# A gathered prefix sum and projection: gathers that convert to FP16 themselves, and stores of two pairs

## The chip, the cores and the metric

The kernel runs on one core of a Trainium2 chip. A time is the time of one execution on the device in microseconds (us); of several runs the median is given. The profile is of one further execution. PE is TensorE, DVE is VectorE, ACT is ScalarE, POOL is GpSimd and SP is SyncE.

## What is computed

```
x: (16, 4096, 512) float32    indices: (16, 2048) int64, sorted    w: (512, 512) float32
gathered = x[b_idx, indices, :]
cs = np.cumsum(gathered, axis=1)
out = np.matmul(cs, w)                      # (16, 2048, 512) float32
```

In each of 16 batches, 2048 rows of 512 numbers are picked, summed up from the first row to each row, and multiplied by one matrix. 67 MB are read by the gathers and 67 MB are written.

## The kernel before, in words

The rows are cut into 256 tiles of 128 rows, 16 to a batch. Two tiles that follow each other make a pair. A tile passes through six steps, each on one engine:

- **gather** (line 127, issued at line 137): POOL issues an indirect DMA. It takes the 128 row numbers from an index tile, reads 128 rows of 2 KB from HBM and writes them as FP32 into one of 16 places (`g32`, eight buffers of a pair). POOL issues the 256 gathers in order, and a gather waits until the place that it fills has been read by a cast.
- **cast** (line 148, the copy at line 152): ACT copies the tile to FP16, into one of 16 places (`g16`, eight buffers of a pair). The first casts take one tile, later ones a pair. The lists made in lines 114 to 122 say which casts stand ahead of which drain on ACT: `far` is how many tiles the casts are ahead of the drains, 2 at the start, more by one every four tiles, up to 10.
- **sums** (line 156, matmuls at line 164): PE multiplies the tile by a triangle of ones, in four matmuls of 128 columns each, so that the sums over the rows of this tile come out transposed in PSUM (`pa`, four buffers).
- **carry** (line 173; line 196, for the first tile of a batch line 183): DVE adds the last column of the tile before and writes FP16 (`cst`, four pairs).
- **project** (line 200, matmuls at line 208): PE multiplies by `w` in four matmuls of 512 columns (`pb`, four buffers). It needs both tiles of its pair, since the rows of a pair are interleaved so that each partition of the output holds two rows that lie side by side in HBM.
- **drain** (line 217, copy at line 220): ACT copies the result from PSUM to SBUF as FP32 (`ob`, eight buffers of a pair).
- **store** (line 222): SP waits for the two drains of a pair and issues one DMA of 512 KB (line 234). The first and the last pair are not interleaved and are stored one tile at a time, 256 KB each (line 229).

What sets the order: each engine works off its own list in order, and semaphores hold it where data or a place is missing. PE's list is written out by hand in lines 338 to 346: sums of a tile are put ahead of projections of older tiles, at most four tiles ahead, fewer at both ends. ACT's list is, for each tile, the casts that are due and then the drain. POOL's list is the gathers alone, SP's the stores alone. The lists of DVE, PE and ACT run as loops over the 16 tiles of a batch, but for the first and last batches, which are written out; POOL's and SP's are written out whole.

Of the kernel before, what the change touches and what calls it, by code (L numbers as in the profile page):

```python
# [7 lines left out]
P = 128  # L8
FP32 = mybir.dt.float32
FP16 = mybir.dt.float16  # L10
# [23 lines left out]
def kernel(  # L34
# [7 lines left out]
    nc = tc.nc  # L42

    B, S, D = x.shape
    N = indices.shape[1]
    R = 2
# [3 lines left out]
    T = B * NT  # L50
    G = T // R
# [2 lines left out]
    FIRST = 2 * R  # L54
    NG = 16
    LEAD = 4
    FAR = 10
    NH = 8
    NA = 4
    NB = 4  # L60
    NC = 4
    NO = 8
    U = NT
    assert U % NG == 0 and U % (R * NO) == 0 and U % NA == 0 and U % (R * NC) == 0 and U % NB == 0
    assert D == 512 and N % (R * P) == 0 and T % P == 0

    x_flat = x.rearrange("b s d -> (b s) d")
# [1 line left out]
    const = ctx.enter_context(tc.tile_pool(name="const", bufs=1))  # L69
# [10 lines left out]
    ident = const.tile([P, P], FP32)  # L80
    zeros = const.tile([P, D], FP16)
    spare = const.tile([P, 1], FP16)
    g32 = [const.tile([P, R, D], FP32, name=f"g32_{i}") for i in range(NG // R)]
    g16 = [const.tile([P, R, D], FP16, name=f"g16_{i}") for i in range(NH)]
    cst = [const.tile([P, DC, R, P], FP16, name=f"cst{i}") for i in range(NC)]
    ob = [const.tile([P, R, D], FP32, name=f"ob{i}") for i in range(NO)]
    pa = [ps.tile([P, DC, R, Q], FP32, name=f"pa{i}") for i in range(NA)]
    pb = [ps.tile([P, D], FP32, name=f"pb{i}") for i in range(NB)]

# [2 lines left out]
    def sem(name):  # L92
        return tc.alloc_semaphore(name)

    s_z, s_ut, s_wc, s_if, s_pt, s_prep, s_of, s_c = (
        sem(f"s_{n}") for n in ("z", "ut", "wc", "if", "pt", "prep", "of", "c")
    )
    s_first = [sem(f"s_first{k}") for k in range(2)]
    s_w = [sem(f"s_w{c}") for c in range(DC)]
    s_idx = [sem(f"s_idx{k}") for k in range(KI)]  # L100
    s_el = [sem(f"s_el{j}") for j in range(R)]
    s_ol = [sem(f"s_ol{j}") for j in range(R)]
    s_g = [sem(f"s_g{i}") for i in range(NG)]
    s_o = [sem(f"s_o{i}") for i in range(NO)]
    s_a = sem("s_a")
    s_d = sem("s_d")
    s_b = sem("s_b")
    s_e = sem("s_e")

    pool, pe, dve, act, sp = (  # L110
        Lane(e) for e in (nc.gpsimd, nc.tensor, nc.vector, nc.scalar, nc.sync)
    )

    casts = []
    cast_by = []
    for u in range(T):
        far = min(FAR, 2 + u // 4, 2 + (T - 1 - u) // 4)
        casts.append([])
        while len(cast_by) <= min(u + far, T - 1):
            n = R if far > 4 and len(cast_by) % R == 0 else 1  # L120
            casts[u].append((len(cast_by), n))
            cast_by += [cast_by[-1] + 1 if cast_by else 1] * n

    for u in range(3 * U, T - 2 * U):
        assert casts[u] == [(t + U, n) for t, n in casts[u - U]]

    def gather(t):
        g, r = divmod(t, R)
        if t >= NG:
            pool.need(s_c, cast_by[R * (g + 1) - NG - 1])  # L130
        if t < FIRST:
            pool.need(s_first[g], 16)
            ap = idx_first[:, t, 0:1]
        else:
            pool.need(s_prep, t // P + 1)
            ap = idxg[:, t // P, t % P : t % P + 1]
        nc.gpsimd.indirect_dma_start(  # L137
            out=g32[g % (NG // R)][:, r, :],
            out_offset=None,
            in_=x_flat,  # L140
            in_offset=bass.IndirectOffsetOnAxis(ap=ap, axis=0),
            element_offset=(t // NT) * S * D,
        ).then_inc(s_g[t % NG], 16)
# [1 line left out]

    PLAIN = (0, G - 1)

    def cast(t, n, first=None):
        g, r = divmod(t, R)
        for u in range(t, t + n):  # L150
            act.need(s_g[u % NG], 16 * (u // NG + 1), first)
        nc.scalar.copy(  # L152
            out=g16[g % NH][:, r : r + n], in_=g32[g % (NG // R)][:, r : r + n]
        ).then_inc(s_c, 1)

    def sums(t, u, first=None):
        g, r = divmod(t, R)
        tiles = None if first is None else R * first
        pe.need(s_c, cast_by[t] if first is None else cast_by[2 * U + t] - 2 * U // R, first)
        pe.need(s_d, t - NA + 1, tiles)  # L160
        for c in range(DC):
            if c == 1 and u is not None:
                pe.need(s_e, u - NB + 1, tiles)
            mm = nc.tensor.matmul(  # L164
                out=pa[t % NA][:, c],
                lhsT=g16[g % NH][:, r, c * P : (c + 1) * P],
                rhs=uq[:] if first is None and g in PLAIN else ut[:],
                start=(c == 0),
                stop=(c == DC - 1),
            )  # L170
        mm.then_inc(s_a, 1)
# [45 lines left out]
    def drain(u, first=None):  # L217
        g, j = divmod(u, R)
        act.need(s_b, u + 1, first)
        nc.scalar.copy(out=ob[g % NO][:, j], in_=pb[u % NB][:]).then_inc(s_e, 1)  # L220

    def store(g):
        b, h = divmod(g, GB)
        rows = out[b, h * R * P : (h + 1) * R * P, :]
        if g in PLAIN:
            for j in range(R):
                sp.need(s_e, R * g + j + 1)
                done = s_ol[j] if g else (s_o[0], s_of)[j]
                nc.sync.dma_start(
                    out=rows[j * P : (j + 1) * P, :], in_=ob[g % NO][:, j]  # L230
                ).then_inc(done, 16)
            return
        sp.need(s_e, R * (g + 1))
        nc.sync.dma_start(
            out=rows.rearrange("(p j) d -> p j d", j=R), in_=ob[g % NO][:]
        ).then_inc(s_o[g % NO], 16)


    with nc.allow_non_contiguous_dma(reason="a few indices, one per partition"):
        for k, eng in enumerate((nc.sync, nc.scalar)):  # L240
            t = k * R
            eng.dma_start(  # L242
                out=idx_first[:, t : t + R, :],
                in_=indices[0, t * P : (t + R) * P]
# [4 lines left out]
    for k in range(KI):  # L249
        nc.sync.dma_start(  # L250
            out=idx64[:, k, :], in_=idx_rows[k * P : (k + 1) * P, :]
        ).then_inc(s_idx[k], 16)
    for c in range(DC):
        eng = (nc.sync, nc.scalar)[c % 2]
        eng.dma_start(out=w32[:, c, :], in_=w[c * P : (c + 1) * P, :]).then_inc(s_w[c], 16)
    for g in range(G):
        store(g)
    for g in range(G - NO, G - 1):
        sp.need(s_o[g % NO], 16 * (g // NO + 1))
    for j in range(R):  # L260
        sp.need(s_ol[j], 16)


    nc.gpsimd.memset(ident[:], 1.0).then_inc(s_ut, 1)
# [3 lines left out]
        out=ident[:],  # L268
        in_=ident[:],
# [7 lines left out]
        out=ut[:],  # L277
        in_=ut[:],
# [9 lines left out]
        out=uq[:],  # L288
        in_=uq[:],
# [6 lines left out]
    for t in range(T):  # L296
        gather(t)
# [15 lines left out]
    for k in range(KI):  # L313
# [3 lines left out]
            out=pb[k % NB][:, :P], in_=idxf[:, k, :], identity=ident[:]  # L317
# [21 lines left out]
    done = 0  # L339
    for u in range(T):  # L340
        lead = min(LEAD, 1 + (u + 2) // 4, 1 + (T - 1 - u) // 6)
        first = u if u // R in PLAIN else u // R * R + R - 1
# [8 lines left out]
    for i in range(head + step, tail):  # L351
        assert order[i] == (order[i - step][0], order[i - step][1] + U)

    def run(i, first=None):
        is_sums, t = order[i]
        after = next((v for k, v in order[i + 1 :] if k != is_sums), None)
        if first is not None:
            t -= 2 * U
            after -= 2 * U
        if is_sums:  # L360
            sums(t, after, first)
        else:
            pe.need(s_wc, DC)
            project(t, after, first)
# [3 lines left out]
    with nc.tensor.Fori(2 * U // R, (T - 2 * U) // R, U // R) as first:  # L368
        pe.new_pass()
        for i in range(head, head + step):  # L370
            run(i, first)
# [7 lines left out]
        act.need(s_w[c], 16)  # L379
        nc.scalar.copy(out=w16[:, c, :], in_=w32[:, c, :]).then_inc(s_wc, 1)  # L380
    def step(u, first=None):
        if u % R == 0:
            if first is None and u == R * NO:
                act.need(s_of, 16)
            act.need(s_o[u // R % NO], 16 * (u // R // NO), first)
        for t, n in casts[u if first is None else 2 * U + u]:
            cast(t if first is None else t - 2 * U, n, first)
        drain(u, first)


    for u in range(2 * U):
        step(u)
# [36 lines left out]
```

## Time and profile before

| what | value |
|---|---|
| median of 5 runs | 353.0 us (352.8 to 353.37) |
| the profiled execution | 353.9 us |
| its span, first to last instruction | 352.2 us |
| granted TensorE clock, mean | 0.985 of full speed |
| DMA, mean over the span | 385 GB/s |
| ACT: casts, and drains | 139 casts, 135.9 us; 256 drains, 138.8 us |
| store of 512 KB, issue to landing, median | 6.8 us |
| store of 256 KB, issue to landing, median | 3.7 us |
| gather, issue to landing, median | 11.1 us |

How to read it: the page has, for each engine, the time in which it was busy, and the same in 40 slices of the span (each digit a tenth). "DMA" is the mean busy share of the 16 DMA engines. A group line names line, engine, operation and tiles, then busy time and mean nanoseconds of one, then how long the engine stood idle ahead of it and what ended that; "issue" there means that no wait is seen. In a timeline line stand start, length, engine, line and operation. The bar of a gather on POOL is the time of its issue; how long the data take is told by the time to landing, from the start of the issue.

### The profile page before, as it was taken

How to read it: one execution, taken by the hardware profiler on the slowest of the kernel's cores; microseconds unless marked ns; L12 is line 12 of the kernel's file. 1: busy time of each engine (PE TensorE's matmuls, PEld its weight loads, DVE VectorE, ACT ScalarE, POOL GpSimd, SP SyncE). 2: the span in 40 equal slices, each digit the busy share in tenths (PEclk: the TensorE clock that was granted, in tenths of full speed). 3: DMA queues.
4: the chain of work that ended last, by engine and by line, in shares of the span. 5: the costliest groups of instructions: out<-in, count | busy, mean ns of one | idle time of the engine just before them, and what ended most of it. 6: DMA issues, size and time to landing. Idle time of an engine off the chain costs nothing.

```text
span 352.2 us, 6498 instructions
## 1 busy us (share of the span) xinstructions
PE 307.5 (87%) x2066; PEld 157.0 (45%) x2066; DVE 179.1 (51%) x263; ACT 262.5 (75%) x399; POOL 244.5 (69%) x266
## 2 busy tenths in 40 slices
PE   7766799998989989898898989889889898999993
PEld 2323355544444444444444544444445444445541
DVE  1443366654555545455454545555545555556541
ACT  2555499777777778777777778678777777879873
POOL 6777777777777777777777777777777777776000
PEclk9998899999999999999999999999999999999998
DMA  7899999999999999999999999999999999999973
GB/s 231 241 320 329 304 313 410 415 412 417 415 415 416 415 415 415 416 414 415 414 415 415 410 410 398 414 408 414 413 412 413 414 414 411 414 414 413 412 298 156
DMA packets 40619, 135.69 MB, mean 385 GB/s; under 512 B 6816, under 2 KB 7072, under 8 KB 40608
## 3 DMA queue, kind: packets, MB, share of 16 engines
q0 software_dynamic: 20480, 67.13, 49.6%
q1 hardware_dynamic: 19568, 67.91, 47.9%
q10 hardware_dynamic: 560, 0.53, 0.5%
q8 instruction: 5, 0.08, 0.1%
q14 instruction: 6, 0.05, 0.1%
HBM read 68.42 MB, written 67.11 MB: 385 GB/s over the span
## 4 chain that ended last, share of the span: by engine, by line
POOL 38%; DMA 21%; PE 16%; issue 14%; ACT 8%; DVE 0%; SPq 0%; ACTq 0%
POOL g L137 38%; DMA g<-in_x_dram,idxg 20%; PE pb L208 12%; ACT g L152 5%; PE pa L164 3%; ACT ob L220 3%; DMA idx<-in_indices_dram 1%; PE pb L304 1%; DVE cst L196 0%; DVE cst L183 0%; PE pb L316 0%; SPq L250 0%; SPq L242 0%; DVE idxf L311 0%; ACTq L26 0%
## 5 line engine op out<-in xcount | busy, mean ns | idle before, releaser
L137 POOL DMA_INDIRECT g<-in_x_dram,idxg x252 | 239.0, 948 | 76.8 <-issue 71.9
L208 PE MATMUL pb<-w,cst 128*128 128x512 f16 x1024 | 264.9, 382 | 1.2 <-DVE cst L196 0.8
L196 DVE TENSOR_TENSOR cst<-pa,cst 128x512 f16<-128x512 f32 x240 | 166.0, 692 | 146.1 <-PE pa L164 145.6
L152 ACT CAST g<-g 128x1024 f16<-128x1024 f32 (+1 forms) x139 | 135.9, 979 | 58.2 <-DMA g<-in_x_dram,idxg 57.5
L220 ACT COPY ob<-pb 128x512 f32<-128x512 f32 x256 | 138.8, 586 | 20.5 <-PE pb L208 20.5
L164 PE MATMUL pa<-ut,g 128*128 128x128 f16 x1008 | 113.4, 222 | 35.6 <-ACT ob L220 23.3
L164 PEld LDWEIGHTS pa<-ut,g 128*128 128x128 f16 x1008 | 73.5, 98 | 116.6 <-ACT ob L220 54.0
L208 PEld LDWEIGHTS pb<-w,cst 128*128 128x128 f16 x1024 | 90.1, 99 | 64.6 <-issue 3.0
L183 DVE CAST cst<-pa 128x512 f16<-128x512 f32 x16 | 11.1, 692 | 13.4 <-PE pa L164 13.4
L304 PE MATMUL pb<-zeros 128*128 128x512 f16 x16 | 7.2, 632 | 1.5 <-DVE zeros L308 1.5
L137 POOL DMA_INDIRECT g<-in_x_dram,idx_first x4 | 4.0, 997 | 1.7 <-issue 0.9
L304 PEld LDWEIGHTS pb<-zeros 128*128 128x128 f16 x16 | 2.3, 150 | 4.8 <-issue 3.3
L380 ACT CAST w<-w 128x512 f16<-128x512 f32 x2 | 1.1, 616 | 3.6 <-DMA w<-in_w_dram 3.6
L377 ACT ACT_TABLE_LOAD x1 | 1.3, 1283 | 2.5 <-issue 2.5
L311 DVE CAST idxf<-idx 128x128 f32<-128x128 uint32 x2 | 0.5, 227 | 4.6 <-DMA idx<-in_indices_dram 4.6
L164 PEld LDWEIGHTS pa<-uq,g 128*128 128x128 f16 x16 | 1.3, 116 | 1.6 <-ACT g L152 0.7
L164 PE MATMUL pa<-uq,g 128*128 128x128 f16 x16 | 1.9, 266 | 0.2 <-ACT g L152 0.2
L316 PE MATMUL pb<-ident,idxf 128*128 128x128 f32 x2 | 0.9, 448 | 0.9 <-DVE idxf L311 0.9
L325 DVE CAST w<-w 128x512 f16<-128x512 f32 x2 | 0.8, 423 | 0.9 <-DMA w<-in_w_dram 0.9
L316 PEld LDWEIGHTS pb<-ident,idxf 128*128 128x128 f32 x2 | 0.4, 206 | 1.7 <-DVE idxf L311 1.5
L308 DVE MEMSET zeros<- 128x256 uint32 x1 | 0.3, 272 | 1.1 <-SPq L90 1.1
L322 DVE CAST idxg<-pb 128x128 uint32<-128x128 f32 x2 | 0.6, 288 | 0.4 <-PE pb L316 0.4
(11 smaller groups left out, 2.1 us busy)
## 6 DMA issues: line engine op xcount, KB each, us to landing
out_dram<-ob SPq DMA_DIRECT2D x126, 512.0 KB, 6.8
g<-in_x_dram,idxg POOLq DMA_INDIRECT x252, 11.1
out_dram<-ob SPq DMA_DIRECT2D x4, 256.0 KB, 3.7
w<-in_w_dram ACTq DMA_DIRECT2D x2, 256.0 KB, 4.2
w<-in_w_dram SPq DMA_DIRECT2D x2, 256.0 KB, 5.2
idx<-in_indices_dram SPq DMA_DIRECT2D x2, 128.0 KB, 3.6
g<-in_x_dram,idx_first POOLq DMA_INDIRECT x4, 4.3
idx_first<-in_indices_dram ACTq DMA_DIRECT2D x1, 2.0 KB, 2.2
```

What stands on the lines that cost most here:

```text
L137: nc.gpsimd.indirect_dma_start(out=g32[g % (NG // R)][:, r, :], out_offset=None, in_=x_flat, in_offset=bass.IndirectOffsetOnAxis(ap=ap, ax ...
L152: nc.scalar.copy(out=g16[g % NH][:, r : r + n], in_=g32[g % (NG // R)][:, r : r + n]).then_inc(s_c, 1)
L164: mm = nc.tensor.matmul(out=pa[t % NA][:, c], lhsT=g16[g % NH][:, r, c * P : (c + 1) * P], rhs=uq[:] if first is None and g in PLAIN else ...
L183: nc.vector.tensor_copy(out=dst, in_=src).then_inc(s_d, 1)
L196: nc.vector.tensor_tensor(out=dst, in0=src, in1=last, op=mybir.AluOpType.add).then_inc(s_d, 1)
L208: mm = nc.tensor.matmul(out=pb[u % NB][:], lhsT=cst[g % NC][:, c, j, :], rhs=w16[:, c, :], start=(c == 0), stop=(c == DC - 1),)
L220: nc.scalar.copy(out=ob[g % NO][:, j], in_=pb[u % NB][:]).then_inc(s_e, 1)
L304: nc.tensor.matmul(out=pb[NB - 1][:], lhsT=zeros[:, :P], rhs=zeros[:], start=True, stop=True)
L316: nc.tensor.transpose(out=pb[k % NB][:, :P], in_=idxf[:, k, :], identity=ident[:]).then_inc(s_pt, 1)
L325: nc.vector.tensor_copy(out=w16[:, c, :], in_=w32[:, c, :]).then_inc(s_wc, 1)
L377: nc.scalar.copy(out=spare[:], in_=zeros[:, :1])
L380: nc.scalar.copy(out=w16[:, c, :], in_=w32[:, c, :]).then_inc(s_wc, 1)
```

## The change

The gathers write FP16: their destination is the FP16 buffer itself, and the DMA converts on the way. The FP32 buffers, the casts on ACT and the lists that placed them are gone. A gather now waits until the sums of the tiles that stood in its place are done, and the sums wait for the gather itself; there are 16 FP16 places as before. The output buffers are four of two pairs instead of eight of one, and SP issues one store of 1 MB for two pairs, but for the first two and the last two pairs, which are stored one by one, with the first and the last pair a tile at a time as before. PE's list, DVE's list and the order of the drains are the same.

```diff
-    FAR = 10
-    NH = 8
...
-    NO = 8
+    W = 2
+    NO = 4
...
-    g32 = [const.tile([P, R, D], FP32, name=f"g32_{i}") for i in range(NG // R)]
-    g16 = [const.tile([P, R, D], FP16, name=f"g16_{i}") for i in range(NH)]
+    g16 = [const.tile([P, R, D], FP16, name=f"g16_{i}") for i in range(NG // R)]
...
-    ob = [const.tile([P, R, D], FP32, name=f"ob{i}") for i in range(NO)]
+    ob = [const.tile([P, W, R, D], FP32, name=f"ob{i}") for i in range(NO)]
...
     def gather(t):
         g, r = divmod(t, R)
-        if t >= NG:
-            pool.need(s_c, cast_by[R * (g + 1) - NG - 1])
+        pool.need(s_a, R * (g + 1) - NG)
...
         nc.gpsimd.indirect_dma_start(
-            out=g32[g % (NG // R)][:, r, :],
+            out=g16[g % (NG // R)][:, r, :],
...
-    def cast(t, n, first=None):
-        g, r = divmod(t, R)
-        for u in range(t, t + n):
-            act.need(s_g[u % NG], 16 * (u // NG + 1), first)
-        nc.scalar.copy(
-            out=g16[g % NH][:, r : r + n], in_=g32[g % (NG // R)][:, r : r + n]
-        ).then_inc(s_c, 1)
-
     def sums(t, u, first=None):
...
-        pe.need(s_c, cast_by[t] if first is None else cast_by[2 * U + t] - 2 * U // R, first)
+        pe.need(s_g[t % NG], 16 * (t // NG + 1), tiles)
...
-        nc.scalar.copy(out=ob[g % NO][:, j], in_=pb[u % NB][:]).then_inc(s_e, 1)
+        nc.scalar.copy(out=ob[g // W % NO][:, g % W, j], in_=pb[u % NB][:]).then_inc(s_e, 1)
...
-        sp.need(s_e, R * (g + 1))
+        sp.need(s_e, R * (g + n))
+        done = {1: s_of, G - W: s_ol}.get(g, s_o[g // W % NO])
         nc.sync.dma_start(
-            out=rows.rearrange("(p j) d -> p j d", j=R), in_=ob[g % NO][:]
-        ).then_inc(s_o[g % NO], 16)
+            out=rows.rearrange("(g p j) d -> p g j d", p=P, j=R),
+            in_=src[:, g % W : g % W + n],
+        ).then_inc(done, 16)
...
-    for g in range(G):
-        store(g)
...
+    for g in range(W):
+        store(g, 1)
+    for g in range(W, G - W, W):
+        store(g, W)
+    for g in range(G - W, G):
+        store(g, 1)
...
-        for t, n in casts[u if first is None else 2 * U + u]:
-            cast(t if first is None else t - 2 * U, n, first)
         drain(u, first)
```

More of the change, by code (lines that the diff above doesn't have):

```diff
@@ L61 @@
     NC = 4
-    NO = 8
+    W = 2
+    NO = 4
     U = NT
-    assert U % NG == 0 and U % (R * NO) == 0 and U % NA == 0 and U % (R * NC) == 0 and U % NB == 0
+    assert U % NG == 0 and U % (W * R * NO) == 0 and U % NA == 0 and U % (R * NC) == 0 and U % NB == 0
     assert D == 512 and N % (R * P) == 0 and T % P == 0
@@ L100 @@
     s_idx = [sem(f"s_idx{k}") for k in range(KI)]
-    s_el = [sem(f"s_el{j}") for j in range(R)]
-    s_ol = [sem(f"s_ol{j}") for j in range(R)]
+    s_ol = sem("s_ol")
     s_g = [sem(f"s_g{i}") for i in range(NG)]
@@ L112 @@
     )
[L114 to L125, printed above, removed]
     def gather(t):
         g, r = divmod(t, R)
-        if t >= NG:
-            pool.need(s_c, cast_by[R * (g + 1) - NG - 1])
+        pool.need(s_a, R * (g + 1) - NG)
         if t < FIRST:
@@ L165, in sums @@
                 out=pa[t % NA][:, c],
-                lhsT=g16[g % NH][:, r, c * P : (c + 1) * P],
+                lhsT=g16[g % (NG // R)][:, r, c * P : (c + 1) * P],
                 rhs=uq[:] if first is None and g in PLAIN else ut[:],
@@ L219, in drain, with store @@
         act.need(s_b, u + 1, first)
-        nc.scalar.copy(out=ob[g % NO][:, j], in_=pb[u % NB][:]).then_inc(s_e, 1)
-    def store(g):
+        nc.scalar.copy(out=ob[g // W % NO][:, g % W, j], in_=pb[u % NB][:]).then_inc(s_e, 1)
+    def store(g, n):
         b, h = divmod(g, GB)
-        rows = out[b, h * R * P : (h + 1) * R * P, :]
+        rows = out[b, h * R * P : (h + n) * R * P, :]
+        src = ob[g // W % NO]
         if g in PLAIN:
@@ L227, in store @@
                 sp.need(s_e, R * g + j + 1)
-                done = s_ol[j] if g else (s_o[0], s_of)[j]
+                done = s_ol if g else (s_o[0], s_of)[j]
                 nc.sync.dma_start(
-                    out=rows[j * P : (j + 1) * P, :], in_=ob[g % NO][:, j]
+                    out=rows[j * P : (j + 1) * P, :], in_=src[:, g % W, j]
                 ).then_inc(done, 16)
             return
-        sp.need(s_e, R * (g + 1))
+        sp.need(s_e, R * (g + n))
+        done = {1: s_of, G - W: s_ol}.get(g, s_o[g // W % NO])
         nc.sync.dma_start(
-            out=rows.rearrange("(p j) d -> p j d", j=R), in_=ob[g % NO][:]
-        ).then_inc(s_o[g % NO], 16)
+            out=rows.rearrange("(g p j) d -> p g j d", p=P, j=R),
+            in_=src[:, g % W : g % W + n],
+        ).then_inc(done, 16)
     with nc.allow_non_contiguous_dma(reason="a few indices, one per partition"):
@@ L255 @@
         eng.dma_start(out=w32[:, c, :], in_=w[c * P : (c + 1) * P, :]).then_inc(s_w[c], 16)
-    for g in range(G):
-        store(g)
[L258 to L261, printed above, removed]
+    for g in range(W):
[4 more added lines that the diff above has]
+        store(g, 1)
+    for i in range(G // W - NO, G // W - 1):
+        sp.need(s_o[i % NO], 16 * (i // NO + 1))
+    sp.need(s_ol, 16 * (R + W - 1))
     nc.gpsimd.memset(ident[:], 1.0).then_inc(s_ut, 1)
@@ L381, in step @@
     def step(u, first=None):
[L382 to L385, printed above, removed]
-        for t, n in casts[u if first is None else 2 * U + u]:
-            cast(t if first is None else t - 2 * U, n, first)
+        if u % (W * R) == 0:
+            if first is None and u == W * R * NO:
+                act.need(s_of, 16 * (R + W - 2))
+            act.need(s_o[u // R // W % NO], 16 * (u // R // W // NO), first)
         drain(u, first)
```

## The prediction

> **What bounds the kernel now.** I read the page's busy shares and slices first, then its groups, then the timeline of POOL, the landings of the gathers in two stretches, the windows of the drains, and last the timeline of ACT near the start and of the end.
>
> ```profile
> PE 307.5 (87%) x2066; PEld 157.0 (45%) x2066; DVE 179.1 (51%) x263; ACT 262.5 (75%) x399; POOL 244.5 (69%) x266
> ...
> POOL 6777777777777777777777777777777777776000
> ...
> DMA  7899999999999999999999999999999999999973
> GB/s 231 241 320 329 304 313 410 415 412 417 415 415 416 415 415 415 416 414 415 414 415 415 410 410 398 414 408 414 413 412 413 414 414 411 414 414 413 412 298 156
> ...
> L137 POOL DMA_INDIRECT g<-in_x_dram,idxg x252 | 239.0, 948 | 76.8 <-issue 71.9
> L208 PE MATMUL pb<-w,cst 128*128 128x512 f16 x1024 | 264.9, 382 | 1.2 <-DVE cst L196 0.8
> ...
> L152 ACT CAST g<-g 128x1024 f16<-128x1024 f32 (+1 forms) x139 | 135.9, 979 | 58.2 <-DMA g<-in_x_dram,idxg 57.5
> L220 ACT COPY ob<-pb 128x512 f32<-128x512 f32 x256 | 138.8, 586 | 20.5 <-PE pb L208 20.5
> ```
>
> POOL looks idle for 31% of the time, but its idle time before a gather is "issue": nothing is waited for. The timeline shows what that is.
>
> ```profile
> 4.72 0.95 POOL L137 DMA_INDIRECT g<-in_x_dram,idx_first  x1 [0.30 <-issue]
> 5.98 0.95 POOL L137 DMA_INDIRECT g<-in_x_dram,idx_first  x1 [0.30 <-issue]
> ...
> 322.99 0.95 POOL L137 DMA_INDIRECT g<-in_x_dram,idxg  x1 [0.30 <-issue]
> ```
>
> A gather is 0.95 us plus 0.30 us, at 5 us, where 231 GB/s flow, as at 323 us, where 413 do. The first starts at 3.28, the last at 322.99: 255 steps of 1.2538 us. So POOL's issue is a fixed pace that nothing on the chip delays. The second bound is level with it: from 60 us on the DMA share is full at 415 GB/s, and a tile's 256 KB in and 256 KB out take 524,288 B / 415 GB/s = 1.263 us.
>
> Then 29.2 us follow the last gather's issue. Where they come from, the landings (least, median and most, gathers of 5 to 20 us, then of 315 us on) and the drains tell (length, busy time and count, clock, DMA share, GB/s):
>
> ```profile
> DMA to landing us min/median/max: 3.6/4.4/5.6
> ```
>
> ```profile
> DMA to landing us min/median/max: 17.0/17.5/17.7
> ```
>
> ```profile
> 20.00:40.00 20.00, 4.69 (x8) 0.87 0.94 322
> 40.00:60.00 20.00, 9.32 (x17) 0.96 0.97 346
> 60.00:100.00 40.00, 16.67 (x32) 1.00 1.03 415
> ```
>
> Eight tiles are drained from 20 to 40 us, while POOL issues sixteen. That deficit is made in a loop through ACT:
>
> ```profile
> 21.93 0.59 ACT L220 COPY ob<-pb 128x512 f32<-128x512 f32 x1
> 22.41 0.62 ACT L152 CAST g<-g 128x512 f16<-128x512 f32 x1
> 24.38 0.59 ACT L220 COPY ob<-pb 128x512 f32<-128x512 f32 x1 [1.35 <-PE pb L208]
> 24.86 0.62 ACT L152 CAST g<-g 128x512 f16<-128x512 f32 x1
> ```
>
> A cast stands behind a drain, the sums behind the cast, the projection behind the sums, the next drain behind that: 2.45 us a tile. The output lags, later stores compete with gathers on a full DMA, and landings go from 4.4 to 17.5 us. The end:
>
> ```profile
> 343.86 0.62 ACT L152 CAST g<-g 128x512 f16<-128x512 f32 x1
> ...
> 344.54 0.40 PE L164 MATMUL pa<-uq,g 128*128 128x128 f16 x4 [0.17 <-ACT g L152]
> ...
> 346.50 1.31 SPq L229 DMA_DIRECT2D out_dram<-ob  x2
> ```
>
> The last gather lands near 340.5, its cast waits 3.4 us for its turn, and from the last sums (344.54) to the end (352.2) are 7.7 us.
>
> **The change, part by part.**
>
> Casts removed. 139 instructions, 135.9 us of ACT, go; ACT keeps 256 drains of 586 ns, about 40% of the span. Nothing of this is on the steady path, as POOL sets that. It counts at the start: without the cast in the loop, PE takes a tile when it has landed. PE's own pace, where it has tiles, is 0.22 for sums and 0.86 for the projection, 1.09 us by the chain, below 1.2538. So the deficit isn't built. Next late is a gather's landing.
>
> Gathers that convert. Reads stay at 67 MB, writes into SBUF halve. The trace of before shows no converting transfer, so two costs are unknown.
> (a) POOL's bar. The 128 rows, and so the addresses to write, are the same; nearest is the row itself, 948 ns. Below: I see no reason for less, as the bar doesn't depend on how transfers go. Above: if the conversion doubles the work per row, 1.9 us. I take 948, being nearest, with no confidence beyond that; the loop for the plain copy may be a better one. Every 10 ns are 2.6 us at the end.
> (b) The engines' time. In the trace's packet records a 4096 B gather packet takes 159 ns at the median, 2048 B loads 84, 1024 B loads 46. If the written bytes count, two rows cost 92; if the read ones, and a packet per row, 168; if the converter is half as fast, some 320. I take 160, about the plain price. The Trainium skill (Collectives: The Full Stack, section The bandwidth ceiling) says that additions within the DMA path cost nothing beyond their reads; that is an addition and not a conversion, no run here shows it, so it only keeps me from taking 320.
>
> The ring. Gathers wait for the sums of 15 tiles before instead of for a cast, and 16 tiles of FP32 plus 16 of FP16 become 16 of FP16. Behind a waiting gather stand all later gathers. 15 tiles are 18.8 us; landing plus sums must fit. At 4.4 to 11 us they do; at the 17.5 of before only just. I put it at nothing as long as (b) holds; without that cover the wait takes POOL's pace down to that of the landings. On PE, the sums' wait moves from cast to landing; the projection behind it is of an older tile and would wait too, until the tile lands.
>
> Stores of two pairs. 126 issues become some 64, in the same row pieces. An output slot is reused after 12 further tiles, 15.0 us; a 512 KB store lands in 6.7 us, one of 1 MB by an estimate (512 KB more at half of 415 GB/s) in 9.2. Covered. The Trainium skill (DMA: Bandwidth & Descriptors, section Rules for kernel authors) wants 1 MiB or more for a transfer, and its section Anatomy of one DMA has a fixed 2.0 us per transfer, which would give some 62 x 2.0 = 124 us for halving the number of stores if they ran one after another. The row decides otherwise: with 512 KB stores the DMA is full at 415 GB/s, the fixed part is hidden, and I give the edit nothing. The bursts may add to a gather's landing; the last two pairs are stored as before, so the end keeps its 7.7 us.
>
> The sum. POOL's last issue stays at 323.0. If the conversion relieves the DMA, landing is 4.4 us and then 7.7: 335.1. If a gather keeps its price, the bytes decide: from 20 to 60 us before moved 13.4 MB and would now move 16.6, 3.2 MB or 7.8 us earlier; the last 29 us moved 8.4 MB at 289 GB/s, which at 415 and with 3.7 us for the last store are 23.9 us, 5.1 less: 352.2 - 12.9 = 339.3. The middle is a span of about 337. The profiled execution took 353.9 against a span of 352.2, and the median of the runs is 353.0, or span plus 0.8. Forecast: 338.
>
> **Rivals.**
> 1. POOL's bar grows (slower). It is the pace, so nothing hides it: 256 x delta. The change has some 15 us to give, so 15 / 256 = 59 ns, 6% of 948, use it up. At a quarter more (237 ns): 338 + 61 = 399. For it: POOL has no slack. Against it: the same number of rows.
> 2. The DMA engines convert at less than the copy's rate (slower). A tile has four gather packets per engine; with 60 ns of slack per tile a packet may take 160 + 15 = 175 ns. At 200: 160 ns a tile, 1.42 us, 256 x 1.42 + 20 = 384. At 320: 1.90 us, about 506, and then POOL waits for sums. For it: the DMA is already full at 1.263 us. Against: fewer bytes are written.
> 3. The change does not relieve what it says: the DMA stays full, and packets of one row (168 ns) and larger stores push landings to 10 us and more: 1.295 us x 256 + 17 = 348, still faster.
>
> **How the numbers follow.** Main case (334 to 344, at 338): 0.47. Rival 3 (344 to 352): 0.09. Rival 1: 0.18, from 355 up, half of it above 400. Rival 2: 0.20, from 355 to 506, two fifths near the double price. A wait on the shorter ring that costs about what is gained: 0.06, a third of it level. The range from 333 to 430 leaves out about 0.17 above and 0.02 below. Both signs hold much, so the likeliest case's own range is 334 to 344. Faster by over 0.2% (the runs spread by 0.16%, so less can't be told from none): 0.56; within: 0.02; slower: 0.42.
>
> **What would show it.** Right: bars of L137's successor at 948 ns with 0.30 before them, the last at 323; landings of 4 to 8 us; about sixteen drains from 20 to 40 us; 12 to 16 us after the last issue. Wrong: a longer bar at once from the first gather (rival 1); gather packets above 175 ns, or waits of POOL for the sums (rival 2); ACT waiting for stores (the slots).

## The result, and the profile after

The changed kernel takes 355.2 us in the median of 42 runs, the kernel before 353.2 in the median of 79 runs taken beside it. The ratio is 1.0051 with a 95% interval of 1.0041 to 1.0061: half a per cent slower. Forecast were 338 us and faster. The profiled execution took 354.2 us, its span is 352.5 (before 352.2). So the profile of after lies at the low end of its runs, and the two spans hardly differ; what differs is where the time is.

From the page of after, the shares of PE, DVE, ACT and POOL, the slices, the queues and the groups that answer to those shown of before:

```profile
PE 302.9 (86%) x2066; PEld 152.4 (43%) x2066; DVE 179.1 (51%) x263; ACT 152.4 (43%) x260; POOL 242.2 (69%) x266
...
POOL 6777777777777777777777777777776777676000
...
DMA  7999999999999999999999999999999999999996
GB/s 190 159 179 288 257 316 290 297 310 295 298 313 290 296 311 298 290 318 296 292 312 291 304 305 305 286 308 309 289 302 307 299 293 314 297 288 319 305 330 243
...
q0 software_dynamic: 36864, 33.57, 58.8%
q1 hardware_dynamic: 18576, 67.90, 50.4%
...
DMA g<-in_x_dram,idxg 53%; POOL g L120 24%; PE pb L183 9%; PE pa L139 4%; DMA idx_first<-in_indices_dram 1%; DVE cst L171 0%; ACT ob L195 0%; SPq L403 0%; SPq L88 0%
...
L120 POOL DMA_INDIRECT g<-in_x_dram,idxg x252 | 236.7, 939 | 80.0 <-issue 66.1
...
L195 ACT COPY ob<-pb 128x512 f32<-128x512 f32 x256 | 149.8, 585 | 189.9 <-PE pb L183 189.9
```

POOL's bar is the same, even 9 ns shorter. ACT has lost its casts and waits. The bytes in SBUF have fallen by a quarter, from 415 GB/s to some 300, and yet the DMA row stays full from end to end: the gathers' queue q0 moved half the bytes that it did before (33.57 MB for 67.13) in a larger share of the engines' time (58.8% for 49.6%), in one packet per row (32768 and 4096 increments) where before a packet held two. The stores' queue q1 moved the same bytes and rose from 47.9 to 50.4%. And the chain that ends last is now the gathers' transfer (53%), where before POOL led with 38%. The lines of before for these readings (queues, and the chain):

```profile
q0 software_dynamic: 20480, 67.13, 49.6%
q1 hardware_dynamic: 19568, 67.91, 47.9%
...
POOL 38%; DMA 21%; PE 16%; issue 14%; ACT 8%; DVE 0%; SPq 0%; ACTq 0%
```

The landings of after (gathers of 5 to 20 us, and of 315 us on), each from the start of the issue:

```profile
DMA to landing us min/median/max: 3.6/4.8/5.8
```

```profile
DMA to landing us min/median/max: 18.9/19.6/20.3
```

Before they went from 4.4 to 17.5 us; now they go to 20.3. Gone is the slow start, as the windows of the drains show (length, busy time and count, clock, DMA share, GB/s):

```profile
20.00:40.00 20.00, 7.71 (x14) 0.96 1.06 234
40.00:60.00 20.00, 9.26 (x16) 1.00 1.14 291
60.00:100.00 40.00, 18.14 (x31) 1.00 1.13 304
```

There are 14 drains from 20 to 40 us where there were eight, but the DMA row is full with 234 GB/s already then. The end, in the timeline (last gather, last sums, last stores):

```profile
323.83 0.94 POOL L120 DMA_INDIRECT g<-in_x_dram,idxg  x1 [0.30 <-issue]
...
344.87 0.39 PE L139 MATMUL pa<-uq,g 128*128 128x128 f16 x4
...
346.77 1.37 SPq L205 DMA_DIRECT2D out_dram<-ob  x2
```

The last gather lands at 323.8 + 20.3 = 344.1, and 8.4 us later all is done. Before it landed near 340.5, and 11.7 us followed. The change took 3.3 us off the tail and put 3.6 on the landings.

### The profile page after: what moved, and what is told of

Its sections match the earlier page's. It is cut to its first block, busy times and chain, and to the rows that moved or that the text cites. A ratio compares the mean times of both kernels' runs of the same rounds, so it can differ in the third digit from the quotient of the medians.

```text
span 352.5 us, 6077 instructions
## 1 busy us (share of the span) xinstructions
PE 302.9 (86%) x2066; PEld 152.4 (43%) x2066; DVE 179.1 (51%) x263; ACT 152.4 (43%) x260; POOL 242.2 (69%) x266
## 3 DMA queue, kind: packets, MB, share of 16 engines
q0 software_dynamic: 36864, 33.57, 58.8%
q1 hardware_dynamic: 18576, 67.90, 50.4%
## 4 chain that ended last, share of the span: by engine, by line
DMA 53%; POOL 24%; PE 12%; issue 9%; DVE 0%; ACT 0%; SPq 0%
DMA g<-in_x_dram,idxg 53%; POOL g L120 24%; PE pb L183 9%; PE pa L139 4%; DMA idx_first<-in_indices_dram 1%; DVE cst L171 0%; ACT ob L195 0%; SPq L403 0%; SPq L88 0%
## 5 line engine op out<-in xcount | busy, mean ns | idle before, releaser
L195 ACT COPY ob<-pb 128x512 f32<-128x512 f32 x256 | 149.8, 585 | 189.9 <-PE pb L183 189.9
L139 PE MATMUL pa<-ut,g 128*128 128x128 f16 x1008 | 99.2, 221 | 40.3 <-DMA g<-in_x_dram,idxg 39.1
L139 PEld LDWEIGHTS pa<-ut,g 128*128 128x128 f16 x1008 | 70.0, 98 | 123.3 <-DMA g<-in_x_dram,idxg 90.9
L285 PE MATMUL pb<-zeros 128*128 128x512 f16 x16 | 5.4, 498 | 1.5 <-DVE zeros L289 1.5
```

Source lines behind the costliest of these rows:

```text
L139: mm = nc.tensor.matmul(out=pa[t % NA][:, c], lhsT=g16[g % (NG // R)][:, r, c * P : (c + 1) * P], rhs=uq[:] if first is None and g in PLAI ...
L195: nc.scalar.copy(out=ob[g // W % NO][:, g % W, j], in_=pb[u % NB][:]).then_inc(s_e, 1)
L285: nc.tensor.matmul(out=pb[NB - 1][:], lhsT=zeros[:, :P], rhs=zeros[:], start=True, stop=True)
```

## The experiments

**Theory A** says that the 16 DMA engines' own time bounds the changed kernel: their time goes by the bytes that they read, which the conversion does not lower, plus something per packet, and there are more packets. **B**: the stores of two pairs do it. **C**: the shorter ring's waits do it (POOL waited 14.0 us for sums, in 36 waits). **D**: HBM does it, whose 67 MB in and 67 MB out are the same in both kernels. Apart from these stands the prediction's claim that the slow start cost the kernel before 7.8 us.

```profile
POOL g L120 <- PE pa L139: 14.0, 36, 1.0
```

The trace also keeps a record of every DMA packet, with its start, its time and the bytes that it wrote. Packet times below are medians of these records.

**conv_w1**, the changed kernel with the stores of before:

```diff
-    W = 2
-    NO = 4
+    NO = 8
...
+    for g in range(G):
+        store(g)
```

> The changed kernel with the stores of before, one pair each. Theory A (the DMA engines' price: a converted row takes 97 ns where a plain one takes 80, and a store packet beside conversions 170 instead of 160): the store packets stay near 170 ns, the time stays at 354 to 356 us. Theory B (the stores of two pairs make the store packets dearer and crowd out gathers): store packets go back to 160 ns, which is 4 x 10.5 x 256 = 10.8 us less, about 344 us.

355.2 us, ratio 1.0048 (1.0029 to 1.0067), as the changed kernel. Its stores' queue took no less, 50.9% (page, queues); the median store packet in the trace's records is 172 ns here as in the changed kernel, and 159 in the kernel before.

```profile
q1 hardware_dynamic: 19568, 67.91, 50.9%
```

**cast_w2**, the kernel before with stores of two pairs (the same edit the other way).

> The kernel before with stores of two pairs only. Theory A: store packets stay at 160 ns, the DMA is full either way, 352.5 to 354 us. Theory B: store packets rise to 170 ns, and the time to about 360 us.

352.7 us, 0.9978 (0.9956 to 1.0001). B falls: the size of the stores is worth nothing that can be told from none, in either kernel, and their packets are dearer only where gathers convert.

**conv_ring32**, 32 places for gathered tiles, with loops over two batches so that each place keeps its semaphore:

```diff
-    NG = 16
+    NG = 32
...
-    U = NT
+    U = 2 * NT
...
-        pe.need(s_g[t % NG], 16 * (t // NG + 1), tiles)
+        pe.need(s_g[t % NG], 16 * (t // NG + 1), first)
```

> The changed kernel with 32 places for gathered tiles instead of 16, so that POOL need not wait for sums. Theory A: POOL issues earlier, but the landings grow by as much; the time stays within 354 to 356 us. Theory C (the shorter ring's waits, 14.0 us in all, set the end): 341 to 345 us.

355.5 us, 1.0064 (1.0042 to 1.0086). POOL's last gather is issued at 320.7 instead of 323.8, and the landings take it all back (gathers of 280 us on, where the changed kernel has 17.8/18.6/20.3):

```profile
DMA to landing us min/median/max: 20.5/22.0/24.4
```

C falls: the ring's waits follow from late landings and do not cause them.

**conv_extra_b and cast_extra_b**, the changed kernel and the kernel before, each with 62 copies of 256 KB from SBUF to SBUF on SP's list:

```diff
     for g in range(W, G - W, W):
         store(g, W)
+        copy()      # nc.sync.dma_start(out=scr[k % 4][:], in_=w32[:, k % DC, :])
```

> The changed kernel with 62 added copies of 256 KB from SBUF to SBUF, again, on a chip where the kernel before takes its usual time. Theory A (the 16 DMA engines' own time is the bound): 128 packets of 2 KB at 84 ns on 16 engines are 0.67 us a copy, some 0.6 by the overlap, 37 us more in all, about 390 us. Theory D (HBM's bytes, the same in both kernels, set the pace): 355 to 360 us.

> The kernel before with the same 62 copies, the control. Theory A: about 391 us. Theory D: 353 to 360 us.

397.8 us (1.1271, 1.1226 to 1.1316) and 392.8 us (1.1137, 1.1091 to 1.1183): 42.6 and 40.3 us more, 0.69 and 0.65 us a copy. (The 42.6 are counted from the 355.2 us of the result above, the 40.3 from runs of the kernel before on the same chip.) D falls. HBM does nothing for these copies, and they cost about what their packets take: 8 packets for each engine, recorded at 96 ns in the changed kernel and at 84 in the kernel before. Theory A had taken 84 for both and so 37 us. The engines have no room in either kernel. The runs that follow change HBM's bytes too, so it is these copies alone that set D aside.

The same two kernels, the next one and cast_far4 also ran on another chip, on which the kernel before took 454.7 us. There the changed kernel with the copies took 416.1 us, the kernel before with them 461.3, and the kernel with half rows (plain_half) 411.4. In these three traces the chain is led by PE (66 to 74%), and the engines stand idle where no releaser is seen ("issue", "remote"), so these times can't be laid to the DMA and are not used for A and D. They do limit the verdict on the change to chips like those of the other runs: here the changed kernel, copies included, is 8% under the kernel before. The changed kernel without copies did not run on that chip, and why the chip is slower stays open.

**plain_half_b**, the changed kernel with plain gathers of 1 KB rows, which write as many bytes as the changed kernel and read half; the sums multiply zeros:

```diff
-    x_flat = x.rearrange("b s d -> (b s) d")
+    x_flat = x.rearrange("b s d -> (b s) d").rearrange("n (h d) -> (n h) d", h=2)
...
-    g16 = [const.tile([P, R, D], FP16, name=f"g16_{i}") for i in range(NG // R)]
+    g16 = [const.tile([P, R, D // 2], FP32, name=f"g16_{i}") for i in range(NG // R)]
...
-                lhsT=g16[g % (NG // R)][:, r, c * P : (c + 1) * P],
+                lhsT=zeros[:, c * P : (c + 1) * P],
```

> The changed kernel with plain gathers of half rows (1 KB read and written per row, no conversion; the sums multiply a tile of zeros, so the gathered numbers are not used). If the conversion and the reads behind it are what fills the engines: POOL's pace, last issue at 321 to 323 us, landings of 4 to 6 us, 335 to 337 us. If it stays above 350: the number of rows or the stores.

338.3 us, 0.9581 (0.9543 to 0.9619). It behaves as the first case of the forecast's sum does (a span of 335.1 us there, 336.6 here). Landings of 280 us on, then POOL's last gather:

```profile
DMA to landing us min/median/max: 2.8/4.7/5.8
```

```profile
322.29 0.95 POOL L120 DMA_INDIRECT g<-in_x_dram,idxg  x1 [0.31 <-issue]
```

The end does lie at POOL's last issue plus some 14 us, if the gathers take less of the engines' time (31.5% by the page's queues, for 58.8%). Three things differ at once here, the bytes read, the packets and the conversion; the next runs part them.

**conv_eighth**, the changed kernel whose stores write 16 of 128 partitions (seven eighths of the output are left out).

> The changed kernel with stores cut to 16 of 128 partitions (seven eighths of the output are not written). If the engines' sum of converted rows and stores is what held the changed kernel (8 x 97 + 4 x 172 ns a tile), it now falls to some 0.8 us a tile, POOL's 1.2435 us is the bound: last issue at 320 to 321, landings of 3 to 5 us, 332 to 335 us. If converting gathers are slow by themselves, landings grow all the same and it stays above 345.

334.9 us, 0.9475 (0.943 to 0.952), landings of 280 us on:

```profile
DMA to landing us min/median/max: 3.5/3.8/4.3
```

Converting gathers with an eighth of the stores keep POOL's pace (last issue at 320.5 us). It is the sum of gathers and full stores that is over it.

**conv_big and plain_big**, which size the conversion by itself: 8 KB are read per index, with conversion to 4 KB and without it, stores again cut to 16 partitions (the output isn't the reference's; plain_big multiplies zeros):

```diff
-    NG = 16
+    NG = 8
...
+    x_flat = x.rearrange("b s d -> (b s) d").rearrange("(n h) d -> n (h d)", h=4)
...
+    g16 = [const.tile([P, R, 4 * D], FP16, name=f"g16_{i}") for i in range(NG // R)]   # plain_big: FP32
```

> Converting gathers by themselves: each index fetches 8 KB (four rows' worth) and writes 4 KB of FP16; stores are cut to 16 of 128 partitions, and the sums use the first quarter of what lands, so the output is not the reference's. 268 MB are read. If a converted row costs a fixed part (97 - 80 = 17 ns each, whatever its length), 8 KB take 320 + 17 ns: 256 gathers x 8 per engine x 0.337 = 690 us. If conversion slows each byte by 21%: 256 x 8 x 0.388 = 795 us. If at half the copy's rate, as in rival 2: 1300 us.

> The counterpart of conv_big without conversion: 8 KB read and 8 KB written in FP32 per index, stores cut to 16 of 128 partitions, sums on a tile of zeros (the output is not the reference's). If a conversion costs a fixed 13 to 20 ns per packet and nothing per byte, the packets are 159 ns per 4 KB (318 for 8) or some 309 if 8 KB go in one, and the whole is within 5% of conv_big, 635 to 665 us. If conversion slows each byte too, plain is 10% or more faster, below 600 us.

667.2 and 674.3 us, two runs each: within 5% of each other as expected, though neither size was met (690, and 635 to 665). The queues' lines of the two pages, conv_big first (packets, MB written, share of 16 engines):

```profile
q0 software_dynamic: 36864, 134.23, 100.4%
```

```profile
q0 software_dynamic: 36864, 268.45, 95.5%
```

32768 of these packets carry data. 100.4% of 16 x 665.3 us are 326 ns for each, 95.5% of 16 x 674.2 us are 314; without the increments, the packet records have 324 and 312 at the median. So a packet that reads 8 KB takes the same time whether 4 or 8 KB are written, but for 12 ns. In these two kernels even that 12 ns doesn't show in the total, as the records of packets overlap more (a DMA share of 1.06 for 1.01).

**cast_ramp**, the kernel before with a faster start:

```diff
-        far = min(FAR, 2 + u // 4, 2 + (T - 1 - u) // 4)
+        far = min(FAR, 4 + u // 4, 2 + (T - 1 - u) // 4)
```

> The kernel before with casts four tiles ahead of the drains from the start instead of two; nothing else. If the prediction's reading of the start is right (the loop drain, cast, sums, projection holds back the output and leaves the DMA unfilled from 20 to 60 us, 7.8 us of traffic), then sixteen instead of eight drains lie between 20 and 40 us and the time falls to 344 to 347 us. If the start is not worth that, 352 to 353 us.

352.4 us, 0.997 (0.995 to 0.9991): 1.2 us less, instead of eight. The windows of its drains:

```profile
20.00:40.00 20.00, 6.58 (x12) 1.00 0.97 351
40.00:60.00 20.00, 6.99 (x13) 1.00 0.99 360
```

Four drains more by 40 us, and four fewer from 40 to 60, so that at 60 us the count is that of before: there the drains lag the landings by the ten tiles that the casts are ahead on ACT's list. So the edit filled the start only in part: twelve drains and not sixteen by 40 us, and by the GB/s 0.9 MB more from 20 to 60 us, not 3.2. At the prediction's rate 0.9 MB are 2.1 us; the interval of the runs allows 0.3 to 1.8, and the last gathers land 2.2 us earlier (15.3 us after the issue instead of 17.5). This run therefore does not test the 7.8 us.

**cast_far4**, casts four tiles ahead throughout (`FAR = 4`, in pairs), meant to take that lag away.

> The kernel before with casts four tiles ahead of the drains throughout, in pairs, instead of up to ten. After the look at the faster ramp I hold that the drains lag the landings by the number of tiles that the casts are ahead, since ACT works in order. Then the lag falls by six tiles, stores begin to fill the DMA 7.6 us earlier, and the time is 345 to 348 us. If the DMA's pace takes it all back, or ACT stalls on landings, 352 us or more.

530.7 us, where 345 to 348 were expected, on the chip where the kernel before took 454.7 (a ratio of 1.17); it was not run on another. The waits in its trace point to the casts, and not only to the chip:

```profile
PEld pa L164 <- ACT g L152: 220.9, 109, 2.1
POOL g L137 <- ACT g L152: 210.1, 116, 6.4
```

With PE's sums four tiles ahead of its projections, casts that are four ahead of the drains stand in the same circle as at the start of the kernel before, now all the way, at some 2 us a tile. Whether a distance of six or seven would gain was not tried.

**cast_w2_ramp**, both edits in the kernel before.

> The kernel before with both edits that were tried alone: stores of two pairs (0.9978) and casts four tiles ahead from the start (0.997). If they add up, 0.995, about 351 us; since the landings set the end in both, no more than that.

352.2 us, 0.9963 (0.9943 to 0.9983). Whether the two add up can't be told, as 0.995 lies within the interval. This version is below both kernels, by 1.6 us against the kernel before and by 3 against the changed one.

## Why the prediction was wrong, point by point

**The step that failed** is the landing of the last gather. The first case of the sum was 323.0 + 4.4 + 7.7 = 335.1 us; the run had 323.8 + 20.3 + 8.4 = 352.5. Of the 17.4 us between them 15.9 are the landing. The second case (339.3) let the landing follow from bytes at 415 GB/s. Two terms were wrong behind it: the reading of why landings grow in the kernel before, and the price of a converting gather. How much is whose can be estimated. In versions with plain gathers the last landings are 15.3 us (cast_ramp) to 17.5 (before). With these, and with the changed kernel's last issue and tail, the sum is 347.5 to 349.7, which is past the 344 of the main case already; the conversion then has the other 3 to 5 us. It is an estimate only: the changed kernel with plain gathers of whole rows, and sums on zeros, was not run.

**POOL's issue**: right. Taken were 948 ns a bar, measured 939; the last issue was put at 323.0 and came at 323.8. Rival 1 did not happen.

**The casts on ACT**: right that PE would take tiles as they land (14 drains from 20 to 40 us), wrong in what that is worth. The sum had 7.8 us for the earlier traffic. By the packet records, with a converting packet counted at the 2 KB that it reads, the changed kernel moved 14.6 MB from 20 to 60 us, where the kernel before moved 13.4 and the sum had 16.6. From 60 to 300 us it then moved less, 96.4 MB for 99.2 (401 GB/s for 413). So what it was ahead by was lost again.

The lag of the stores did cost something, in the tail. From 313 us on, the kernel before is held by PE, which works almost without a pause at 1.09 us a tile behind a gather that landed at 311.68. The chain of 300 us on:

```profile
by line: PE pb L208 48.2%; DMA g<-in_x_dram,idxg 30.6%; PE pa L164 11.1%; ACT ob L220 3.3%; issue 2.2%; DVE cst L196 1.3%; ACT g L152 1.1%; ACTq L393 0.1%; ACTq L26 0.1%
```

Its last cast waits 3.4 us; with the casts gone the tail is 3.3 us shorter, where the sum had 5.1.

**The landings**: here the prediction misread the view that it showed. It took the growth from 4.4 to 17.5 us for stores competing after a slow start, and set 1.263 us a tile by bytes as the DMA's pace. The trace gives another pace. In the chain of the kernel before stand these two gathers, 190 tiles apart (start and time to landing):

```profile
57.45 7.57 DMA g<-in_x_dram,idxg
...
295.44 16.24 DMA g<-in_x_dram,idxg
```

They landed at 65.02 and 311.68, so landings come every 246.66 / 190 = 1.298 us. That pace is not that of the sixteen engines together. In the trace each gather has 16 increments of its semaphore, as many as there are engines, and each is read here as the end of one engine's share. In the kernel before, the fifteenth increment comes 8.1 us after the issue for gathers of 60 to 120 us and 6.3 for those of 280 us on (medians), while the sixteenth goes from 8.7 to 16.2. So fifteen stay on POOL's pace and the last falls behind, which fits one engine that is late throughout; the trace doesn't name the engine. In the changed kernel the fifteenth goes from 8.9 to 17.7 us, only some 1.2 ahead of the last. There all of them are late.

**Gathers that convert, term (b)**: it took "160, about the plain price" for two rows, and let the case that fewer written bytes relieve the DMA stand in its sum. Measured are some 97 ns a row (96 or 98), 194 for two, and 172 for a store packet beside them instead of 159. Of the 35 ns between 159 and 194, 9 come from one row to a packet (2 x 84 for a packet of 2 KB, which the prediction had as 168), the rest from 13 ns on every packet, which conv_big and plain_big show as fixed (12 ns on 8 KB).

Not all recorded time is lost, as records overlap. An engine's packets of one tile record 8 x 97 + 4 x 172 = 1464 ns, and 8 x 159 = 1272 in the kernel before, both without increments. The copies show the overlap: 8 packets of 96 ns cost 0.69 us, and 8 of 84 cost 0.65, so the recorded time is 1.12 and 1.03 times the cost. By this estimate an engine needs some 1.31 us a tile in the changed kernel and 1.23 in the kernel before, on either side of the 1.24 to 1.25 us of POOL. The landings agree: from 9.8 us (gathers of 60 to 120 us) they grow to 18.6 (280 us on), a pace of 1.308 us.

So the mechanism is that of rival 3, with 20 us where it had ten for the last landing. That its 1.295 us a tile lies so near is luck in part: it had neither the 13 ns nor the overlap. It also held the change to be faster still. That bytes not written are bytes saved is refuted by conv_big and plain_big: half the bytes written, and 1% less time.

**The ring**: the price of nothing holds (conv_ring32), although POOL did wait 14.0 us; with twice the places POOL issues 3 us earlier and gains nothing, as landings are the bound.

**Stores of two pairs**: nothing, as given (conv_w1, cast_w2). From the last sums to the end are 7.6 us, for 7.7. The 2.0 us that the prediction took from the Trainium skill (DMA: Bandwidth & Descriptors, section Anatomy of one DMA) is given there for transfers that POOL issues; these stores are SP's, and no run here shows a fixed part of theirs. The prediction set the figure aside, so nothing hangs on it.

**Rival 2** had the right place and too high a price. Both of its signs came: two rows were over 175 ns in the records (194), and POOL waited for sums. But its pace of 1.42 us at 200 ns left the overlap of packets out.

What the runs leave open: what the 13 ns are, how much of them an engine really loses, and why one increment of the sixteen is late in the kernel before.

## What to carry to other kernels

A DMA that converts spares the engine that did the cast, not the DMA: here its engines' time went by the bytes read, with a part for each packet. Where the DMA is full it gains nothing. (On the slower chip the converting kernel was the faster one; what it spared there is not shown.) Where landings grow steadily through a trace, work out the pace from two of them before giving an earlier start any worth; if that pace is above the issuer's, the landings set the pace, and a lag of the work behind them shows in the tail (3.3 us here). And a full "DMA" row with fewer GB/s is no sign of room: added traffic that no one waits for (62 copies here) shows at once whether there is any.

## What the runs showed of the hardware

- Conversion from FP32 to FP16 within a gather had no price per byte that shows: 324 ns for 8 KB read and 4 KB written against 312 for 8 KB both ways. The Trainium skill (Collectives: The Full Stack, section The bandwidth ceiling) says the like of additions within the DMA; these two runs show it for a conversion, but for 12 ns a packet.
- Beside converting gathers most other packets are recorded 12 or 13 ns longer (medians): stores of 4 KB 172 for 159 ns, semaphore increments of the changed kernel 22 for 9, added copies of 2 KB 96 for 84.
- Plain gathers of 2 KB rows go two to a packet, plain ones of 1 KB four to a packet (8192 packets of 4 KB in plain_half_b), converting ones one to a packet.
- At the end of the kernel before (landings of 280 to 330 us) the last of a gather's 16 increments came 9.6 us after the fifteenth. The Trainium skill (DMA: Bandwidth & Descriptors, section Latency and other measured facts) says that engines 7 and 15 are usually the slow ones; no run here tells which engine it was.
